# A hybrid DeltaNet and window-attention layer: rounds of an inverse spread over more steps, value copies in two halves, and a lasting slot for wide weights

## The chip, the cores and the metric

One core of one Trainium2 chip runs the whole layer in one launch. The metric is the device time of a run in microseconds (us); the kernel before takes 1549.96 us, the median of 3 runs (1548.43 to 1550.71).

## The reference, cut to what matters

One layer on 1024 latent tokens and 256 context tokens, width 1024, in float32. It projects all tokens once and sends the columns to two groups.

```python
px = modulate(rms_norm(x, norm1_w), sh1, sc1) @ w_in          # latents; pc the same for the context
# group A, gated DeltaNet: short_conv + SiLU on q, k, v; q and k L2-normalised;
#   per head, direction and chunk of 64 tokens a triangular solve, then a scan over chunks
m = where(strict, einsum(kb, k) * decay, 0);  a_mat = I + m
u = triangular_solve(a_mat, v * beta);  w = triangular_solve(a_mat, kb * exp(gam))
# group B, neighbourhood attention on a 16 x 64 grid: q, k RMS-normed per head (weights na_q, na_k);
#   each query sees an 8 x 16 window and all context keys, with a learned 2-D bias
x = x + g1 * (concat(dn_x, na_x) @ w_out)
x = x + g2 * swiglu(modulate(rms_norm(x, norm2_w), sh2, sc2), w_ffn_in, w_ffn_out)
```

## The kernel before, in words

The projection stage, up to about 600 us, is a list of jobs run one behind another. Each job is a group of columns of the input projection, and its matmuls (float32 split in a high and a low part, so three products: hh by whi, hl by whi, hh by wlo) fill TensorE. Then come the scan and the rest of the attention, the output projection and the FFN, which the change does not touch.

There are two kinds of job. A `Block` makes 128 columns over all its tokens: `k`, `q`, `v` of group A, `nk` and `nq` of group B. Its result stands in up to three of four `blk` banks; ScalarE copies it out (`evac`, L438 and L453), VectorE and ScalarE do convolution taps and SiLU (L457 to L468), and `norm` and `finish` do sums over heads and transposes for the next stage. A `Wide` job makes 256 or 272 columns, token tile by token tile: `z1`, `nv0`, `nv1`, and at the end `z0`. Its weights are loaded in two halves through one buffer `wraw`, cast by ScalarE into the tile `zw` (L587).

The jobs in order: k0 to k3, z1, nk0, nk1, nk2, nv0, nk3, q0 to q3, nq0 to nq3, v0, nv1, v1, v2, v3, z0.

Beside the jobs runs a background program (`bg`), which is advanced by one step after each of eight parts of a block's matmuls, and by two or three steps after each tile of a wide job. First it computes the inverses of the triangular 32 x 32 matrices of all chunks (`block_inverses`): thirty rounds on VectorE over a tile `N` (L885 and L887), then transposes of `N` on TensorE (L897), then products that are stored in DRAM as `x_d`. Then come the `preps`, ten of them in eight steps each, which read `x_d` (as `xc`) and the products of keys `kk_d`, and put decay factors (`rg` on GpSimd, L957; `pr` on TensorE, L967) on them. Preps from the third on wait until all q jobs are finished.

The text order is not the engines' order: a scheduler places each engine's instructions by its own rules, so a step that is handed out elsewhere changes what stands in front of what on all five queues. All loads and most stores are issued by SyncE, in the order of its queue.

Three more names. In `norm` of an nk job, a sum over heads (L492) is made in three segments, each followed by Ln on ScalarE (L493); all take a bank of the tag `m`. The normalised nk keys go to DRAM as `nk_d`, the nv values as `nv_d` and from there, copied in window order, as `vw_d` (L1108); v goes to `v_d` (L535). The first attention pair reads `qs`, `kh`, `kl` (L303) and is handed out among the tiles of z0.

Of the kernel before, what the change touches and what calls it, by code (L numbers as in the profile page):

```python
# [20 lines left out]
KT = 8  # L21
# [67 lines left out]
def hybrid(ctx, tc, a, dbg):  # L89
# [45 lines left out]
        dve.memset(bias[:, i:i + 1], v)  # L135
    b_eps, b_naq = bias[:, 0:1], bias[:, 1:2]
    mr = const("mr", [128, 5, 128], F32R)
    mneg = const("mneg", [128, 2, 128], F32R)

    v_d = dram.tile([T, 512], F32, name="v_d", tag="v_d")  # L140
    k_d = dram.tile([T, 512], F32, name="k_d", tag="k_d")
# [233 lines left out]
    with ExitStack() as bs:  # L375
# [32 lines left out]
        class Block:  # L408
# [64 lines left out]
            def norm(self):  # L473

                kind, acc, t0, i = self.kind, self.acc, self.t0, self.i
                if kind == "v":
                    return
                if kind == "k":
                    sp.dma_start(kT_d[:, :, i], acc.rearrange("p (c t) -> p c t", t=128))
                    return  # L480
                r = self.r
                if kind == "q":
                    sp.dma_start(qT_d[:, :, i], acc[:, t0:].rearrange("p (c t) -> p c t", t=128))
                    p = bank()
                    for c in range(8):
                        pe.matmul(p[:, c:c + 1], r[:, t0 + c * 128:t0 + (c + 1) * 128], M[C_ONE][:, 0:1],
                                  start=True, stop=True)
                    dve.tensor_copy(SQ[:, :, i], p[:, 0:8])
                    return
                for s0, n in self.segs:  # L490
                    p = bank()
                    pe.matmul(p[:, :n], M[C_BD2], r[:, s0:s0 + n], start=True, stop=True)  # L492
                    act.activation(r[:, s0:s0 + n], p[:, :n], AF.Ln, bias=b_eps, scale=1.0 / ND)  # L493
                if kind == "nq":
                    act.activation(r[:, t0:], r[:, t0:], AF.Exp, scale=-0.5, bias=b_naq)
                else:
                    act.activation(r[:, t0:], r[:, t0:], AF.Exp, scale=-0.5)
                isk = kind == "nk"
                u = acc
                dve.scalar_tensor_tensor(u[:, t0:], u[:, t0:], qkw[:, isk:isk + 1], r[:, t0:],  # L500
                                         op0=OP.mult, op1=OP.mult)
                hl16 = cp.tile([128, 2, T], F16, name="hl16", tag="kx", bufs=3)
                h16, l16 = hl16[:, 0], hl16[:, 1]
                if isk:
                    act.copy(h16, u)
                    dve.tensor_tensor(l16, u, h16, OP.subtract)
                else:
                    for hf in range(2):
                        s = slice(t0 + hf * 512, t0 + hf * 512 + 512)
                        uv = u[:, s].rearrange("p (r b c) -> p b r c", r=8, b=4)  # L510
                        hv, lv = (x[:, s].rearrange("p (b r c) -> p b r c", b=4, r=8) for x in (h16, l16))
                        act.copy(hv, uv)
                        dve.tensor_tensor(lv, uv, hv, OP.subtract)
                for i, x in enumerate((h16, l16)):
                    for hb in range(2):
                        hd = 2 * self.i + hb
                        dst = nk_d[i, hd] if isk else nq_d[hd, i]
                        sp.dma_start(dst, x[hb * 64:hb * 64 + 64, t0:])

            def finish(self):  # L520
                kind, acc, i = self.kind, self.acc, self.i
                if kind in "kv":
                    vt = cp.tile([128, NCH, 128], F32, name="vt", tag="kx", bufs=3)
                    for g, m in ((0, 4), (4, 4), (8, 2)):
                        p = bank()
                        for c in range(m):
                            pe.transpose(p[:, c * 128:(c + 1) * 128], acc[:, (g + c) * 128:(g + c + 1) * 128], ident)
                        if kind == "k":
                            act.copy(vt[:, g:g + m].rearrange("p c d -> p (c d)"), p[:, :m * 128])
                        else:  # L530
                            dve.tensor_tensor(vt[:, g:g + m], p[:, :m * 128].rearrange("p (c d) -> p c d", d=128),
                                              SV[:, g:g + m, i:i + 1].to_broadcast([128, m, 128]), OP.mult)
                        yield
                    dst = v_d if kind == "v" else k_d
                    sp.dma_start(dst[:, i * 128:(i + 1) * 128].rearrange("(c p) d -> p c d", p=128), vt)  # L535
                if kind == "q":
                    kT = cp.tile([128, T], F32, name="kTh", tag="kx", bufs=3)
                    sp.dma_start(kT.rearrange("p (c t) -> p c t", t=128), kT_d[:, :, i])
# [25 lines left out]
        class Wide:  # L564


            def __init__(self, kind, half, zp):
                self.kind, self.half, self.zp = kind, half, zp
                self.n = 272 if kind == "z" and half else 256
                self.lasting = kind == "z" and not half  # L570

            def room(self):
                w = self.zp().tile([128, 2, KT, 256 if self.lasting else 272], F32R, name="zw", tag="zw")
                self.hi, self.lo = w[:, 0], w[:, 1]

            def prefetch(self):
                h2, n = 2 * self.half, self.n // 2
                src = a["w_nv"] if self.kind == "nv" else a["w_z%d" % self.half]
                if self.kind == "z":
                    h2 = 0  # L580
                if not self.lasting:
                    self.room()
                for i in range(2):
                    raw = wp.tile([128, KT, 136], F32, name="wraw", tag="wraw", bufs=1)
                    r, s = raw[:, :, :n], slice(i * n, i * n + n)
                    sp.dma_start(r, src[h2 + i])
                    act.copy(self.hi[:, :, s], r)  # L587
                    pool.tensor_tensor(self.lo[:, :, s], r, self.hi[:, :, s].bitcast(F32), OP.subtract)
# [55 lines left out]
        with ExitStack() as xs:  # L644
# [65 lines left out]
            with tc.manual_schedule(engines={mybir.EngineType.PE, mybir.EngineType.DVE, mybir.EngineType.Activation}):  # L710
# [30 lines left out]
                for k in range(1, KT):  # L741
# [11 lines left out]
                                ada(q, act.copy)  # L753
                    if k == 5:
                        act.copy(mr[:, 4], ident)
                        for d in range(2):
                            act.mul(mneg[:, d], masks[:, d], -1.0e30)
                        act.copy(mr[:, 0:4], masks)

        cp = pools(bs, "cp", "right")  # L760
        late = ExitStack()
        adp = pools(late, "adp", "left")
        zpool = [pools(late, "zp", "left")]
        first_half = ExitStack()
        cpa = pools(first_half, "cpa", "left")
        WK = cpa.tile([128, 2, NU, 32], F32, name="WK", tag="WK")
        KKc = WK[:, 1]

        def zp():
            return zpool[0]  # L770

        def decay_tables(gp):
            def small(name):
# [51 lines left out]
        def block_inverses():  # L825
            with ExitStack() as gs:
# [55 lines left out]
                for c in range(30, 0, -1):  # L882
# [2 lines left out]
                    dve.tensor_tensor(t, N[:P, :, 0:c, c:c + 1].to_broadcast([P, 4, c, w]),  # L885
                                      N[:P, :, c:c + 1, c + 1:32].to_broadcast([P, 4, c, w]), OP.mult)
                    dve.tensor_tensor(N[:P, :, 0:c, c + 1:32], N[:P, :, 0:c, c + 1:32], t, OP.add)  # L887
                    if c % 2:
                        yield
                flat = N.rearrange("p b r c -> p b (r c)")  # L890
                dve.memset(flat[:P, :, 0:1024:33], 1.0)
                yield
                U = WK.rearrange("p d u i -> p (d u) i")
                for i0 in range(0, 32, 4):
                    p = bank()
# [21 lines left out]
        def preps():  # L917

            first_half.close()
            with ExitStack() as gs:  # L920
# [28 lines left out]
                def prep(i, got):  # L949
# [9 lines left out]
                    for d, c, kk, xc, at in got:  # L959
                        for q in q32:  # L960
                            act.copy(fxs[d][q, :, q], xc[q, 1])
                    yield 1
                    es = []
                    for d, c, kk, xc, at in got:
                        p = bank("pr")
# [61 lines left out]
                        yield  # L1027
                flush(tick[0] + 2)

        jobs = first + [Block("k", 2), Block("k", 3), Wide("z", 1, zp)]  # L1030
        inv = len(jobs)
        jobs += [Block("nk", i) for i in range(3)] + [Wide("nv", 0, zp), Block("nk", 3)]
        turn = len(jobs)
        jobs += [Block("q", i) for i in range(4)]
        later = len(jobs)
        queries = range(turn, later)
        jobs += [Block("nq", i) for i in range(4)] + [Block("v", 0), Wide("nv", 1, zp)]
        values = len(jobs) - 1
        jobs += [Block("v", i) for i in (1, 2, 3)] + [Wide("z", 0, zp)]

        def blk(n):
            return jobs[n] if 0 <= n < len(jobs) and isinstance(jobs[n], Block) else None
# [9 lines left out]
        for n in range(2, len(jobs) + 2):  # L1052
# [7 lines left out]
            if n == len(jobs) - 2:  # L1060
                bg.drain()
                bg2.drain()
                late.close()
                sp1 = pools(middle, "sp1", "left")
                zpool[0] = sp1
                jobs[n + 1].room()
                fill = attention(pools(attn, "nw", "left", 2))
                next(fill)
            if final:
# [21 lines left out]
            elif j:  # L1091
                for k in range(KT):
                    j.mm([k])
                    if k >= 3:
                        next(fin, 0)
                    bg.step(1)
                    if n > inv + 4:
                        bg2.step(1)
# [1 line left out]
            for _ in fin:  # L1100
                pass
            done.add(n - 2)
            if isinstance(j, Wide) and n == values:
                vlat = nv_d[CT:].rearrange("(r c) d -> r c d", c=64)
                for cb in range(4):
                    for ch in range(4):
                        for r in range(4):
                            sp.dma_start(vw_d[r * 32:r * 32 + 32, :, cb, ch],  # L1108
                                         vlat[4 * ch + r, BLKS[cb]:BLKS[cb] + 32].rearrange("c (h d) -> c h d", d=128))
            if nrm:  # L1110
                nrm.norm()
            if isinstance(j, Block):
# [665 lines left out]
```

## Time and profile before

| | |
|---|---|
| median of 3 runs | 1549.96 us |
| profiled execution | 1549.54 us |
| its span | 1547.5 us |
| TensorE busy | 1479.8 us (96%) |
| VectorE, ScalarE, GpSimd busy | 994.3, 727.7, 233.6 us |
| inverse's rounds on VectorE | to 258.5 us |
| q0 to q3 | 249.6 to 342.8 us |
| nv1 | 437.7 to 494.6 us |
| v1, v2, v3 | 496.6 to 548.5 us |

The time of a run is that of the span and 2.0 us around it. In the rows of the profile a row begins with the line of the kernel and the engine, `out<-in` are the names of the tiles, and the arrow in brackets names what ended the idle time in front of an instruction.

### The profile page before, as it was taken

The page shows a single profiled execution, that of the slowest core. Times are in us where ns is not written, and L with a number is a line of the kernel's source. Part 1 is how long each engine was busy: PE and PEld are TensorE (multiplying, and loading weights), DVE is VectorE, ACT ScalarE, POOL GpSimd, SP SyncE. Part 2 cuts the span into 40 slices and gives each one's busy share as a digit, 9 for nine tenths or more (in the row PEclk, how much of TensorE's full clock was granted, in tenths as well). Part 3 has the DMA queues.
Part 4 walks back from the last instruction along what each step waited for, and adds up shares of the span by engine and source line. Part 5 has one row for each costly group of instructions (what it writes and reads, how often), then busy time and mean ns, then how long its engine had stood idle before and what let it go on. Part 6 is the DMA issues. An engine that isn't in the chain of part 4 may idle for free. (4 is left out here: it accounts for less than half of the span.)

```text
span 1547.5 us, 23963 instructions
## 1 busy us (share of the span) xinstructions
PE 1479.8 (96%) x8702; PEld 1235.2 (80%) x8702; DVE 994.3 (64%) x1712; ACT 727.7 (47%) x1404; POOL 233.6 (15%) x286
## 2 busy tenths in 40 slices
PE   6999999899989978999999999999999999999998
PEld 3788787678778867888887878888888888888887
DVE  5774497675554543777986469866665556599652
ACT  5442552635764235666773166333333334354440
POOL 1154500733554010111210000000000000000000
PEclk9999999999999979999999999999999999999999
DMA  9274221577556467899637502632323324698742
GB/s 389 64 217 133 67 72 63 163 212 241 182 169 212 130 174 237 283 288 261 220 102 255 208 34 82 211 102 103 103 102 103 109 100 159 231 381 279 244 144 82
DMA packets 204118, 267.35 MB, mean 173 GB/s; under 512 B 16736, under 2 KB 114528, under 8 KB 202976
## 3 DMA queue, kind: packets, MB, share of 16 engines
q1 hardware_dynamic: 198480, 261.07, 51.7%
q10 hardware_dynamic: 5520, 4.76, 0.9%
q8 instruction: 68, 1.11, 0.3%
q14 instruction: 50, 0.41, 0.1%
HBM read 201.02 MB, written 68.94 MB: 174 GB/s over the span
## 5 line engine op out<-in xcount | busy, mean ns | idle before, releaser
L405 PE MATMUL blk<-hh,whi 128*128 128x512 f32 (+1 forms) x410 | 123.4, 395 | 2.3 <-ACT kk L550 1.4
L1415 ACT CAST uhi<-wq 128x512 fp32r<-128x512 f32 x101 | 61.0, 622 | 133.5 <-issue 84.6
L1415 ACT CAST uhi<-ws 128x512 fp32r<-128x512 f32 x91 | 53.9, 621 | 147.3 <-PE ps L1354 92.9
L405 PE MATMUL blk<-hl,whi 128*128 128x512 f32 (+1 forms) x410 | 116.8, 377 | 0.3 <-DVE hl L707 0.3
L595 PE MATMUL blk<-zw,hh 128*128 128x256 f32 (+1 forms) x576 | 115.0, 293 | 1.3 <-ACT kk L550 1.1
L405 PE MATMUL blk<-hh,wlo 128*128 128x512 f32 (+1 forms) x410 | 114.7, 377 | 0.6 <-POOL wlo L200 0.6
L1416 DVE TENSOR_TENSOR ulo<-wq,uhi 128x512 fp32r<-128x512 f32 x101 | 67.4, 687 | 59.1 <-ACT uhi L1415 34.0
L1354 PE MATMUL ps<-hT,uhi 128*128 128x512 f32 x336 | 103.7, 390 | 0.0
L1354 PE MATMUL ps<-hT,ulo 128*128 128x512 f32 x336 | 103.5, 389 | 0.0
L1354 PE MATMUL ps<-lT,uhi 128*128 128x512 f32 x336 | 103.4, 389 | 0.0
L595 PEld LDWEIGHTS blk<-zw,hh 128*128 128x128 f32 x576 | 92.8, 192 | 5.2 <-ACT kk L550 1.4
L1354 PE MATMUL ps<-hB,uhi 128*128 128x512 f32 x288 | 89.2, 391 | 0.6 <-ACT hB L1529 0.6
L1354 PE MATMUL ps<-lB,uhi 128*128 128x512 f32 x288 | 88.7, 389 | 0.4 <-DVE lB L1530 0.4
L1354 PE MATMUL ps<-hB,ulo 128*128 128x512 f32 x288 | 88.7, 389 | 0.0
L405 PEld LDWEIGHTS blk<-hh,wlo 128*128 128x128 f32 x410 | 72.6, 192 | 15.3 <-POOL wlo L200 0.9
L405 PEld LDWEIGHTS blk<-hl,whi 128*128 128x128 f32 x410 | 72.4, 191 | 14.5 <-DVE hl L707 0.8
L405 PEld LDWEIGHTS blk<-hh,whi 128*128 128x128 f32 x410 | 69.4, 194 | 18.2 <-issue 4.5
L595 PE MATMUL blk<-zw,hl 128*128 128x256 f32 (+1 forms) x288 | 83.2, 289 | 0.0
L1354 PEld LDWEIGHTS ps<-lT,uhi 128*128 128x128 f32 x336 | 63.1, 188 | 13.1
L1354 PEld LDWEIGHTS ps<-hT,ulo 128*128 128x128 f32 x336 | 63.1, 188 | 13.1
L1354 PEld LDWEIGHTS ps<-hT,uhi 128*128 128x128 f32 x336 | 62.9, 188 | 13.0
L200 POOL TENSOR_TENSOR wlo<-wraw,whi 128x1024 fp32r<-128x1024 f32 x18 | 44.7, 2485 | 179.2 <-ACT whi L199 160.7
(359 smaller groups left out, 3540.5 us busy)
## 6 DMA issues: line engine op xcount, KB each, us to landing
wq<-w_fo SPq DMA_DIRECT2D x99, 256.0 KB, 4.2
wq<-w_gu SPq DMA_DIRECT2D x88, 256.0 KB, 2.9
wad<-wa SPq DMA_DIRECT2D x64, 256.0 KB, 4.4
bt<-rpb SPq DMA_DIRECT2D x64, 192.0 KB, 3.8
t_d<-g SPq DMA_DIRECT2D x22, 512.0 KB, 3.6
fr<-t_d SPq DMA_DIRECT2D x44, 256.0 KB, 5.0
f_d<-g SPq DMA_DIRECT2D x33, 256.0 KB, 2.1
fr<-f_d SPq DMA_DIRECT2D x33, 256.0 KB, 3.8
```

Of the source, the lines that this page charges most:

```text
L200: lo_engine.tensor_tensor(o, r, h.bitcast(F32), OP.subtract)
L405: pe.matmul(o, ww[:, k], xx[k][:, s], start=k == 0 and j == 0, stop=k == KT - 1 and j == 2)
L595: pe.matmul(p[:, :c1 - c0], x[k][:, s], ww[:, k, c0:c1], start=k == 0 and j == 0, stop=k == KT - 1 and j == 2)
L1354: pe.matmul(o, w[wi][:, k], x[xi][:, k], start=first and k == 0 and j == 0, stop=k == n - 1 and j == 2, skip_group_check=True)
L1415: act.copy(hi, self.raw[key])
L1416: dve.tensor_tensor(lo, self.raw[key], hi.bitcast(F32), OP.subtract)
```

## The change

Eight edits. (1) The rounds of the inverse are handed out one a step, not two. (2) Four empty steps, in place of one, stand before the transposes of `N`, and the first prep gets one empty step before its first sums. (3) In `norm`, the third segment's sum takes a bank of the tag `pr`. (4) The copies to `vw_d` are made in two halves, one of two heads behind nv0 and one behind nv1, each of 64 copies. (5) The store of `v_d` is issued by ScalarE. (6) The tile `zw` is taken from a pool that lasts, opened early, always at its full width. (7) The product `mneg` is made later, in another pool. (8) The last `finish` of the q jobs marks its job done as soon as its steps are through.

```diff
                 for j, (s0, n) in enumerate(self.segs):
-                    p = bank()
+                    p = bank("pr" if j == 2 else "m")
...
-                    sp.dma_start(dst[:, i * 128:(i + 1) * 128].rearrange("(c p) d -> p c d", p=128), vt)
+                    (act if kind == "v" else sp).dma_start(dst[:, i * 128:(i + 1) * 128].rearrange("(c p) d -> p c d", p=128), vt)
...
             def room(self):
-                w = self.zp().tile([128, 2, KT, 256 if self.lasting else 272], F32R, name="zw", tag="zw")
+                w = sp1.tile([128, 2, KT, 272], F32R, name="zw", tag="zw")
...
-                if not self.lasting:
-                    self.room()
+                self.room()
...
+        sp1 = pools(middle, "sp1", "left")
         adp = pools(late, "adp", "left")
-        zpool = [pools(late, "zp", "left")]
+        mneg = adp.tile([128, 2, 128], F32R, name="mneg", tag="mneg")
+        for d in range(2):
+            act.mul(mneg[:, d], mr[:, d].bitcast(F32), -1.0e30)
...
-                    if c % 2:
-                        yield
+                    yield
                 flat = N.rearrange("p b r c -> p b (r c)")
                 dve.memset(flat[:P, :, 0:1024:33], 1.0)
-                yield
+                for _ in range(4):
+                    yield
...
                     yield 1
+                    if i == 0:
+                        yield 1
...
-                    if k >= 3:
-                        next(fin, 0)
+                    if k >= 3 and next(fin, 0) == 0:
+                        done.add(n - 2)
...
-            if isinstance(j, Wide) and n == values:
+            if isinstance(j, Wide) and j.kind == "nv":
+                hv = slice(2 * j.half, 2 * j.half + 2)
...
-                            sp.dma_start(vw_d[r * 32:r * 32 + 32, :, cb, ch],
-                                         vlat[4 * ch + r, BLKS[cb]:BLKS[cb] + 32].rearrange("c (h d) -> c h d", d=128))
+                            rows = vlat[4 * ch + r, BLKS[cb]:BLKS[cb] + 32].rearrange("c (h d) -> c h d", d=128)
+                            sp.dma_start(vw_d[r * 32:r * 32 + 32, hv, cb, ch], rows[:, hv])
```

What moves, first on SyncE's queue around nv0. Before, with the load of q2's weights (`wraw<-w_conv`) in the fifth row:

```order
L518 DMA nk_d<-hl_1621 64x1280 x4
L195 DMA wraw<-w_conv 128x8x128
L518 DMA nk_d<-hl_1794 64x1280 x4
L518 DMA nk_d<-hl_1992 64x1280 x4
L195 DMA wraw<-w_conv 128x8x128
L907 DMA x_d<-WK 128x1280
L910 DMA x_d<-ut 128x1280
```

And now the same place, from q1's weights on:

```order
L194 DMA wraw<-w_conv 128x8x128
L517 DMA nk_d<-hl_1788 64x1280 x4
L1104 DMA vw_d<-nv_d 32x2x128 x22
L517 DMA nk_d<-hl_1970 64x1280 x2
L1104 DMA vw_d<-nv_d 32x2x128
L517 DMA nk_d<-hl_1970 64x1280 x2
L1104 DMA vw_d<-nv_d 32x2x128 x41
L194 DMA wraw<-w_conv 128x8x128
L902 DMA x_d<-WK 128x1280
L194 DMA wraw<-w_conv 128x8x128
L905 DMA x_d<-ut 128x1280
```

All 64 copies of the first half stand in front of q2's weights and of the first `x_d` store, and q3's weights between the two `x_d` stores.

Then ScalarE's queue from v1's evacuation (`cr<-blk`) on. Before:

```order
L453 COPY cr<-blk 128x512 x2
L1001 COPY y_2232<-pr 32x4x96
L468 ACT_TABLE_LOAD
L468 ACTIVATE cacc<-cacc 128x1280
L453 COPY cr<-blk 128x256
L453 COPY cr<-blk 128x512 x2
L468 ACTIVATE cacc<-cacc 128x1280
L453 COPY cr<-blk 128x256
L453 COPY cr<-blk 128x512 x2
L587 CAST zw<-wraw 128x8x128
```

Now:

```order
L452 COPY cr<-blk 128x512 x2
L584 CAST zw<-wraw 128x8x128
L467 ACT_TABLE_LOAD
L467 ACTIVATE cacc<-cacc 128x1280
L452 COPY cr<-blk 128x256
L452 COPY cr<-blk 128x512 x2
L467 ACTIVATE cacc<-cacc 128x1280
L584 CAST zw<-wraw 128x8x128
L534 DMA v_d<-vt 128x10x128
L452 COPY cr<-blk 128x256
L452 COPY cr<-blk 128x512 x2
```

The first cast of z0's weights stood behind v3's evacuation; it stands now between v1's and v2's, and the store of `v_d` has come to this queue.

Last, TensorE at the end of v3 (the last `blk<-` of L405 before, L404 now). Before:

```order
L405 MATMUL blk<-hh_458,wlo 128x256
L405 MATMUL blk<-hh_458,wlo 128x512 x2
L303 LDWEIGHTS qs
L303 MATMUL sc<-kh,qs 128x256
L303 LDWEIGHTS qs
L303 MATMUL sc<-kh,qs 128x256
```

Now:

```order
L404 MATMUL blk<-hh_457,wlo 128x256
L404 MATMUL blk<-hh_457,wlo 128x512 x2
L592 MATMUL blk<-zw,hh_128 128x256
L592 MATMUL blk<-zw,hl_129 128x256
L592 MATMUL blk<-zw,hh_128 128x256
L592 MATMUL blk<-zw,hh_130 128x256
```

The first scores of the attention (`sc`) came right behind v3; now 96 matmuls of z0, four token tiles, stand between.

More of the change, by code (lines that the diff above doesn't have):

```diff
@@ L137, in hybrid @@
     mr = const("mr", [128, 5, 128], F32R)
-    mneg = const("mneg", [128, 2, 128], F32R)
     v_d = dram.tile([T, 512], F32, name="v_d", tag="v_d")
@@ L489, in norm @@
                     return
-                for s0, n in self.segs:
-                    p = bank()
+                for j, (s0, n) in enumerate(self.segs):
+                    p = bank("pr" if j == 2 else "m")
                     pe.matmul(p[:, :n], M[C_BD2], r[:, s0:s0 + n], start=True, stop=True)
@@ L564, in hybrid, with __init__ @@
         class Wide:
-            def __init__(self, kind, half, zp):
-                self.kind, self.half, self.zp = kind, half, zp
+            def __init__(self, kind, half):
+                self.kind, self.half = kind, half
                 self.n = 272 if kind == "z" and half else 256
-                self.lasting = kind == "z" and not half
             def room(self):
-                w = self.zp().tile([128, 2, KT, 256 if self.lasting else 272], F32R, name="zw", tag="zw")
+                w = sp1.tile([128, 2, KT, 272], F32R, name="zw", tag="zw")
                 self.hi, self.lo = w[:, 0], w[:, 1]
@@ L755, in hybrid @@
                         act.copy(mr[:, 4], ident)
-                        for d in range(2):
-                            act.mul(mneg[:, d], masks[:, d], -1.0e30)
                         act.copy(mr[:, 0:4], masks)
@@ L767, in hybrid @@
         KKc = WK[:, 1]
-        def zp():
-            return zpool[0]
         def decay_tables(gp):
@@ L1028, in preps @@
                 flush(tick[0] + 2)
-        jobs = first + [Block("k", 2), Block("k", 3), Wide("z", 1, zp)]
+        jobs = first + [Block("k", 2), Block("k", 3), Wide("z", 1)]
         inv = len(jobs)
-        jobs += [Block("nk", i) for i in range(3)] + [Wide("nv", 0, zp), Block("nk", 3)]
+        jobs += [Block("nk", i) for i in range(3)] + [Wide("nv", 0), Block("nk", 3)]
         turn = len(jobs)
@@ L1036, in hybrid @@
         queries = range(turn, later)
-        jobs += [Block("nq", i) for i in range(4)] + [Block("v", 0), Wide("nv", 1, zp)]
+        jobs += [Block("nq", i) for i in range(4)] + [Block("v", 0), Wide("nv", 1)]
         values = len(jobs) - 1
-        jobs += [Block("v", i) for i in (1, 2, 3)] + [Wide("z", 0, zp)]
+        jobs += [Block("v", i) for i in (1, 2, 3)] + [Wide("z", 0)]
         def blk(n):
@@ L1063, in hybrid @@
                 late.close()
-                sp1 = pools(middle, "sp1", "left")
-                zpool[0] = sp1
-                jobs[n + 1].room()
                 fill = attention(pools(attn, "nw", "left", 2))
```

## The prediction

> **What bounds the kernel now.** The page comes first: TensorE is busy for nearly the whole span.
>
> ```profile
> span 1547.5 us, 23963 instructions
> PE 1479.8 (96%) x8702; PEld 1235.2 (80%) x8702; DVE 994.3 (64%) x1712; ACT 727.7 (47%) x1404; POOL 233.6 (15%) x286
> ```
>
> So time is won or lost only as TensorE idle time (67.7 us in all) or as a lower granted clock. Busy time by stretches says where (start:end, length, PE busy, then the other engines, PEclk, DMA share, GB/s):
>
> ```profile
> 140.00:260.00 120.00, 109.54 (x638) 92.93 (x637) 91.29 (x112) 49.64 (x79) 35.29 (x27) 0.98 0.21 60
> 260.00:345.00 85.00, 77.42 (x437) 61.93 (x436) 53.91 (x51) 42.71 (x73) 39.12 (x42) 0.89 0.56 176
> 345.00:497.00 152.00, 143.28 (x1045) 119.31 (x1044) 84.49 (x106) 90.24 (x169) 72.69 (x88) 1.00 0.66 205
> 497.00:612.00 115.00, 98.71 (x679) 83.47 (x678) 52.35 (x83) 44.83 (x79) 12.27 (x21) 0.90 0.58 171
> ```
>
> The change moves nothing outside 140 to 612 us that TensorE waits for. Idle in the four stretches: 10.5, 7.6, 8.7 and 16.3 us. The clock takes (1 - 0.89) x 85 = 9.4 us in 260:345 and 0.10 x 115 = 11.5 us in 497:612. What TensorE waits for, in windows 140:300, 300:500 and 500:612 (total us, times, longest):
>
> ```profile
> PE m L492 <- ACT cr L493: 5.3, 4, 1.4
> PE pr L967 <- POOL rg L957: 2.9, 3, 1.2
> PE m L897 <- DVE N L891: 2.9, 1, 2.9
> ...
> PE pr L998 <- DVE y L1000: 1.9, 1, 1.9
> PE m L219 <- DVE acc L234: 1.5, 1, 1.5
> ...
> PE sc L303 <- DVE mx L305: 5.1, 2, 4.1
> PE sc L303 <- DMA kh<-nk_d: 4.5, 1, 4.5
> ...
> ```
>
> The short waits cost more than their length, since half clock follows some of them. The first of these stretches begins right behind the wait of 1.5 us (L219), the second in the wait for kh; the clock is the third number from the end:
>
> ```profile
> 330.50:333.80 3.30, 3.30 (x9) 2.62 (x10) 3.14 (x5) 0.00 (x0) 0.00 (x0) 0.50 0.81 242
> 552.40:569.30 16.90, 9.71 (x43) 7.54 (x44) 11.95 (x18) 6.74 (x10) 3.06 (x3) 0.50 0.87 246
> ```
>
> I price such a stretch at 1.7 us (half of some 3.3), or at 3.4 where the wait is long enough for two of them. The Trainium skill (TensorE: Matmul & The Clock Gate, HAM oscillation) says that it takes an idle gap of over some 3.4 us to lose the clock. The rows disagree: 1.5 us was enough once. By that rule the query stretch would lose no clock, before or after, except behind the one wait of 5 us below, and the sum would be about 1.7 us worse than mine.
>
> **Part 1, nk sums and the inverse (140 to 260 us).** The third of three sums (L492) gets a bank of its own and no longer waits for the Ln of the first: 5.3 us in four places, three of them before 235 us (4.0 us), one at 273. But behind them stands L897, which waits for VectorE, and VectorE has no room:
>
> ```profile
> 196.00:258.00 62.00, 56.48 (x368) 49.75 (x366) 59.38 (x63) 23.93 (x34) 5.46 (x2) 1.00 0.21 60
> ```
>
> Its 59.4 busy us of 62 are the rounds of the inverse, instruction after instruction, and their order is unchanged. Only the first of the four waits lies before the rounds begin, so the rounds end at most 1.3 us earlier; I take 1.2. The transposes also come three 512-column matmuls later in TensorE's row, 0.7 us of work that now covers part of their wait. **Gain 1.9 us**, not 4.0; the wait at L897 itself grows.
>
> **Part 2, queries (260 to 345 us).** Splitting the values puts 64 more copies vw_d<-nv_d behind nv0. There are still 64 of them behind nv1, each half as large: 128 copies in place of 64. SyncE's price for issuing one (ns min/median/max):
>
> ```profile
> L1108 SPq DMA_DIRECT2D vw_d<-nv_d x64: 469/596/1811, 461.0 to 531.4; - x64
> L940 SPq DMA_DIRECT2D kk<-kk_d x20: 320/462/1326, 285.1 to 482.0; - x20
> L195 SPq DMA_DIRECT2D wraw<-w_conv x10: 540/593/658, 32.8 to 442.0; - x10
> 525.61 6.36 SPq L1108 DMA_DIRECT2D vw_d<-nv_d  x10
> ```
>
> In a row they come every 0.64 us (ten in 6.36). What half a copy costs no row shows. The bounds are 0.47 (its own minimum; kk's median is 0.46) and 0.64. Issue time does not follow size: 512 KB of wraw take 593 ns, 64 KB of vw_d 596, 256 KB of kk 462. So I take **0.64, the price of a whole one**; the lower end is a rival. In the new order q2's weights wait for all 64:
>
> ```profile
> nv_d<-zt ACTq DMA_DIRECT2D x20, 128.0 KB, 2.3
> wraw<-w_conv SPq DMA_DIRECT2D x10, 512.0 KB, 3.8
> ...
> 236.12 0.33 ACTq L606 DMA_DIRECT2D nv_d<-zt  x1
> ...
> 253.36 0.59 SPq L195 DMA_DIRECT2D wraw<-w_conv  x1
> 269.49 1.04 ACT L199 CAST whi<-wraw 128x1024 fp32r<-128x1024 f32 x1 [4.61 <-PE blk L405]
> 270.44 1.07 ACT L453 COPY cr<-blk 128x512 f32<-128x512 f32 x2
> 270.61 2.37 POOL L200 TENSOR_TENSOR wlo<-wraw,whi 128x1024 fp32r<-128x1024 f32 x1 [17.27 <-ACT whi L199]
> 271.54 4.77 DVE L457 TENSOR_SCALAR cacc<-cr,cw 128x1024 f32<-128x1024 f32 x1 [3.59 <-ACT cr L453]
> 284.99 2.05 DVE L461 SCALAR_TENSOR_TENSOR cacc<-cr,cw,cacc 128x1022 f32<-128x1022 f32 x1
> ...
> 273.84 1.92 POOL L931 MEMSET y<- 128x512 f32 x4
> ...
> 269.02 0.39 PE L405 MATMUL blk<-hl,whi 128*128 128x512 f32 x1
> 269.24 0.62 PE L405 MATMUL blk<-hh,wlo 128*128 128x512 f32 x2
> ...
> 275.22 1.28 ACT L497 ACT_TABLE_LOAD   x1
> ```
>
> The last store of nv0 is issued at 236.1, about 3.0 earlier with part 1 (4.0 of waits gone, 1.0 given back to an earlier transpose that waits for VectorE), and lands 2.3 later: 235.4. The first block of sixteen copies waits for that one; 49 copies remain, 49 x 0.64 = 31.4, and four nk_d stores stand among them, 2.4 at the same price. The load goes out at 269.2 instead of 253.4 and lands at 273.0. ScalarE's cast of it stood at 269.5, or 267.6 with part 1: **5.4 us late**, and everything queued behind it on ScalarE with it: the evacuation cr<-blk of q0, the Ln of the sums, then on VectorE the taps, on GpSimd wlo and rg. The three places where TensorE meets this chain, in its new order:
> - L219, 30 matmuls into q1. Matmuls of 512 columns start every 0.23 us (two of 0.39 in 0.62), so 7 us after q1's start at some 268.6 (270.6 less 1.9): 275.6. It needs a bank that the Ln frees: cast at 273.0 (1.0), two copies (1.1), table load (1.3), two Ln (1.1): 277.5, or 1 us more with the third: **2 to 4 us late**, 3 taken.
> - L486 (q0's squares) has moved to 8 matmuls into q2. Before, the taps ran from 271.5 to 287.0, 15.5 us, 3 of them for two other steps of the inverse that now come later. So 12.5 from 275.5, then table load, silu and square (1.3 + 1.1 + 1.1): 291.5 at most, and 288.5 if wlo disturbs the first tap less than before. TensorE is there at 278.6 + 4.2 (the rest of q1) + 1.9 = 284.7: 4 to 6.5 us; 5 taken.
> - L967 (first preps) has moved from the end of q1 to 22 matmuls into q2, but GpSimd now makes q3's wlo (2.4) and six memsets (2.9) before rg's four pieces. 2 to 5 us; 3 taken, in place of the 2.9.
>
> New waits 11; old ones that go 1.3 + 2.9 + 1.5 and, taken half, 1.9: 6.6. One half-clock stretch more: 1.7. **Loss 6.1 us** (3 to 9). The mask product computed earlier (mneg) and the four empty steps cost nothing: GpSimd, ScalarE and the steps' owners have slack there, and the work is the same.
>
> **Part 3, 345 to 497 us.** Preps 2 to 9 start later and end three steps earlier. The same instructions meet 8.7 us of idle; **0, at most 3 either way**.
>
> **Part 4, values to the first attention pair (497 to 612 us).**
>
> ```profile
> 495.00 0.33 ACTq L606 DMA_DIRECT2D nv_d<-zt  x1
> ...
> 535.68 0.61 SPq L586 DMA_DIRECT2D wraw<-w_z  x1
> 545.47 0.37 SPq L535 DMA_DIRECT2D v_d<-vt  x1
> ...
> 532.78 1.35 ACT L453 COPY cr<-blk 128x256 f32<-128x256 f32 x3 [3.34 <-PE blk L405]
> ...
> 541.09 1.27 ACT L468 ACTIVATE cacc<-cacc 128x1280 f32<-128x1280 f32 x1 [6.96 <-DVE cacc L461]
> ...
> 549.35 1.07 ACT L587 CAST zw<-wraw 128x1024 fp32r<-128x1024 f32 x1
> ...
> wraw<-w_z SPq DMA_DIRECT2D x1, 512.0 KB, 4.7
> ```
>
> Before, SyncE sat from 536.3 to 545.5 waiting to store v_d, and kh came late behind it: the 4.5 us. Now that store is ScalarE's, and z0's first half stands ahead of the first pair in TensorE's row, so the 4.5 goes, and of the waits for mx behind it I keep 2.0. The new wait: ScalarE's first zw cast has moved ahead of the evacuation of v2, and it needs w_z. That load stands behind 48 copies that need the last nv_d: 495.0 + 2.3 + 48 x 0.64 + 1 (two stores among them) + 3.7 (the six stores from 532.0 to 535.7) = 532.7, landed at 537.4. Cast 1.1, table load 1.3, silu 1.3, first copy 0.4: 541.5. TensorE is done with v2 as its evacuation starts, at 533, and v3 needs v2's banks: **8.5 us of stall**, and 3.4 for the clock behind it. Clock in the pair 1.7 (8.5 before). The pair's idle time is 16.9 - 9.7 = 7.2 in the row of half clock above and 3.9 of the 4.5 that lie before it; the rest of the stage, 5.2 idle and 3.0 clock, stays. Sum 8.5 + 3.4 + 2.0 + 1.7 + 8.2 = 23.8 against 16.3 + 11.5 = 27.8: **gain 4.0 us** (0 to 8). The moved store of v_d stands on ScalarE ahead of v3's evacuation; what it stores is v1's, finished while v3 runs, so it holds nothing up (at worst 1 to 2 us, since two of v3's three banks are read behind it).
>
> **Sum** against the profiled execution, 1549.54 us (span 1547.5 and 2.0 around it; the median is 0.4 more): -1.9 + 6.1 + 0 - 4.0 = +0.2. Forecast **1550 us**, no change, by two large terms that cancel; its own range is 1543 to 1557.
>
> **The rivals.**
> - *The half copies issue at 0.48.* For: kk's and vw_d's own shortest. Against: the median, and that wraw, eight times the size, costs the same. Then q2's load goes out 49 x 0.16 = 7.8 earlier, in time for the cast, and the three new waits fall to what stood there before (part 2: 0). w_z lands 7.7 earlier, the stall falls to 0.8 without its clock, and part 4 gains 4.0 + 7.7 + 3.4 = 15.1. With part 1, 17 less; I take 15 to 16, **1534 us**. It decides from about 0.55 downward.
> - *SyncE's queue is slower than the steady pace, and each wait behind it draws half clock.* For: the 64 copies hold outliers up to 1.8 us, 1.2 over the median. Against: the median is at the steady pace. Two such outliers in each run of 48 put 2.4 on q2's load and 2.4 on w_z, and two more half-clock stretches cost 3.4: 8.2 more, **1558 us**. It decides from a mean of 0.69 upward, seen as waits at L486 and at v3's first matmul of over 7 and 10 us.
> - *The change does nothing that TensorE sees* (banks and queues give way elsewhere): within 3 us of before, part of the forecast.
>
> **How the numbers follow.** Forecast 0.50, fast copies 0.22, slow queue 0.28. The range reaches to both rivals, 1536 to 1560. A measurement of this kernel tells 0.2%, 3.1 us, from no change. Of the forecast's 0.50 I put 0.14 under 1546.9, 0.21 within and 0.15 over. Faster 0.36, same 0.21, slower 0.43.
>
> **What would show it.** Right: L492 gone from the waits; L897's wait over 3.5 us; vw_d's median issue near 600 ns with 128 of them; new waits at L486 and L219 (their lines shifted by a few) of 3 to 6 us; a stall of 8 to 9 us between v2 and v3 released by ScalarE's evacuation; no wait for kh. Wrong: a vw_d median under 530 ns, or no stall at v3, makes it 10 to 15 us faster; a wait at the second w_z half, or preps that end later than nv1, makes it slower than all of this.

## The result, and the profile after

The changed kernel takes 1541.36 us, the median of 20 runs, against 1549.66 us: 0.9952 of before, 95% interval 0.9941 to 0.9963. It is 8 us faster where no change was forecast. In the profiled execution, 1541.49 us, the page begins:

```profile
span 1539.4 us, 24029 instructions
PE 1474.1 (96%) x8702; PEld 1231.0 (80%) x8702; DVE 993.6 (65%) x1712; ACT 728.2 (47%) x1405; POOL 234.8 (15%) x286
```

The stretches of before, in the same columns (length, PE busy, the other engines, then PEclk, DMA share, GB/s), and one more:

```profile
140.00:260.00 120.00, 109.50 (x642) 92.93 (x641) 92.12 (x115) 49.59 (x78) 35.36 (x27) 0.97 0.26 73
260.00:345.00 85.00, 80.58 (x467) 64.25 (x466) 64.93 (x57) 44.90 (x76) 41.69 (x42) 0.94 0.66 203
345.00:497.00 152.00, 143.80 (x1062) 119.91 (x1062) 75.17 (x102) 95.43 (x180) 74.41 (x95) 0.98 0.64 196
497.00:612.00 115.00, 101.37 (x741) 87.42 (x740) 52.73 (x95) 45.76 (x91) 12.00 (x16) 0.97 0.59 172
612.00:915.00 303.00, 293.91 (x2249) 251.14 (x2248) 212.11 (x565) 177.97 (x443) 32.64 (x65) 1.00 0.67 209
```

The queries lose 4.4 us to waits (7.6 before) and 0.06 x 85 = 5.1 to the clock (9.4 before). From v1 to the first attention pairs it is 13.6 (16.3) and 3.5 (11.5); some of that moved on, since 612:915 holds 9.1 us of idle time where before held 5.1. Counted between the same matmuls instead: from nk0's first to v2's last 387.0 us (391.6), from there to the scan's first product with `vk` (L1229, L1234 before) 74.7 (78.3). So 4.6 us came from the part up to v2's last matmul and 3.6 from the part behind it.

What TensorE waits for in 140:260, 260:345 and 500:612:

```profile
PE m L892 <- DVE N L885: 5.7, 1, 5.7
...
PE pr L964 <- POOL rg L952: 2.7, 4, 0.9
PE pr L984 <- DVE kk L971: 1.1, 1, 1.1
PE m L485 <- ACT cr L470: 0.2, 1, 0.2
...
PE blk L404 <- ACT cr L452: 5.3, 1, 5.3
PE sc L313 <- DVE bt L308: 2.6, 2, 1.8
```

The sums are gone and the wait for the rounds has grown to 5.7. The waits of 3 and 5 us forecast among the queries are not there (0.2 at L485). The new stall at v3 is there, 5.3 us and not 8.5. SyncE's and ScalarE's timelines around nv0 and q2's weights, and SyncE's price of a copy (ns min/median/max), say why:

```profile
215.42 14.71 SPq L1104 DMA_DIRECT2D vw_d<-nv_d  x22
...
231.46 0.64 SPq L1104 DMA_DIRECT2D vw_d<-nv_d  x1
...
233.42 27.31 SPq L1104 DMA_DIRECT2D vw_d<-nv_d  x41
260.83 0.59 SPq L194 DMA_DIRECT2D wraw<-w_conv  x1
...
234.83 0.37 ACT L602 COPY zt<-blk 128x256 f32<-128x256 f32 x1 [3.48 <-DMA vw_d<-nv_d]
238.06 0.34 ACTq L603 DMA_DIRECT2D nv_d<-zt  x1
...
269.17 1.05 ACT L198 CAST whi<-wraw 128x1024 fp32r<-128x1024 f32 x1 [0.58 <-PE blk L404]
...
L1104 SPq DMA_DIRECT2D vw_d<-nv_d x128: 529/595/1690, 215.4 to 521.3; - x128
```

A half copy costs what a whole one did (595 and 596 ns), as forecast. But 23 of the 64 go out while nv0 still runs, and the others do not wait for the last store at 238.06. The load goes out at 260.8, and ScalarE's cast of it waits for TensorE, not for the load. The last store itself did not come 3.0 us earlier, as forecast, but 1.9 later than before (236.12): the profile has ScalarE wait 3.48 us, in front of the copy that feeds it, for the landing of copies to `vw_d`. No wait of TensorE in 140:260 is put down to that. The end of nv1 and v3, on both queues:

```profile
490.92 30.98 SPq L1104 DMA_DIRECT2D vw_d<-nv_d  x46
...
525.45 0.61 SPq L583 DMA_DIRECT2D wraw<-w_z  x1
...
530.57 1.05 ACT L584 CAST zw<-wraw 128x1024 fp32r<-128x1024 f32 x1 [13.89 <-DMA wraw<-w_z]
531.64 1.28 ACT L467 ACT_TABLE_LOAD   x1
532.93 1.27 ACT L467 ACTIVATE cacc<-cacc 128x1280 f32<-128x1280 f32 x1
534.11 1.33 ACT L452 COPY cr<-blk 128x256 f32<-128x256 f32 x3
```

The chain is the forecast one (46 copies, load, cast, table, silu, first copy of v2's banks), only it begins at 490.9 and not behind the last nv_d store, forecast to land at 497.3. The 46 copies take 0.67 us each, under the 0.69 from which the rival of the slow queue decides.

### The profile page after: what moved, and what is told of

Read it like the earlier page. It is cut to its first block, busy times and chain, and to the rows that moved or that the text cites. A ratio compares the mean times of both kernels' runs of the same rounds, so it can differ in the third digit from the quotient of the medians.

```text
span 1539.4 us, 24029 instructions
## 1 busy us (share of the span) xinstructions
PE 1474.1 (96%) x8702; PEld 1231.0 (80%) x8702; DVE 993.6 (65%) x1712; ACT 728.2 (47%) x1405; POOL 234.8 (15%) x286
## 5 line engine op out<-in xcount | busy, mean ns | idle before, releaser
L404 PE MATMUL blk<-hh,whi 128*128 128x512 f32 (+1 forms) x410 | 123.0, 394 | 6.8 <-ACT cr L452 5.3
L404 PE MATMUL blk<-hl,whi 128*128 128x512 f32 (+1 forms) x410 | 115.4, 375 | 0.3 <-DVE hl L704 0.3
L404 PE MATMUL blk<-hh,wlo 128*128 128x512 f32 (+1 forms) x410 | 114.6, 375 | 0.6 <-POOL wlo L199 0.6
L404 PEld LDWEIGHTS blk<-hh,whi 128*128 128x128 f32 x410 | 69.0, 194 | 21.9 <-ACT cr L452 6.1
L404 PEld LDWEIGHTS blk<-hl,whi 128*128 128x128 f32 x410 | 72.5, 192 | 14.9 <-DVE hl L704 0.8
L404 PEld LDWEIGHTS blk<-hh,wlo 128*128 128x128 f32 x410 | 72.5, 192 | 14.9 <-POOL wlo L199 0.9
```

The source lines that it names most:

```text
L404: pe.matmul(o, ww[:, k], xx[k][:, s], start=k == 0 and j == 0, stop=k == KT - 1 and j == 2)
```

## The experiments

All are timed against before; the changed kernel stands at 0.9952. The first four undo one edit each.

**The bank of the third sum** (`x_pr`): `bank("pr" if j == 2 else "m")` becomes `bank()`.

> The changed kernel with one edit undone: the third sum of norm takes a bank of the tag m again. Theory A (the gain in front of v2's end, 4.6 us, comes mostly from the background steps being handed out later; three of the four waits at the sums are swallowed by the wait for the inverse's rounds): the four waits of 1.2 to 1.4 us come back, the wait for the rounds shrinks by as much, 1 to 2 us slower than the changed kernel, ratio to before 0.996. Rival B (the bank is the gain there): 4 to 5 us slower, ratio 0.998.

1541.91 us, 0.9953 (0.9935 to 0.9972). Theory A, since B's 0.998 lies outside. Its waits in 140:300:

```profile
PE m L491 <- ACT cr L492: 5.2, 4, 1.4
...
PE m L892 <- DVE N L885: 2.2, 1, 2.2
```

The 5.2 us of sums come back, and the wait for VectorE's rounds falls from 5.7 to 2.2. The bank is worth nothing that these runs can tell.

**The steps** (`x_yield`):

```diff
-                    yield
+                    if c % 2:
+                        yield
...
-                for _ in range(4):
-                    yield
+                yield
...
-                    if i == 0:
-                        yield 1
```

> The changed kernel with the steps undone: two rounds of the inverse a step, one empty step in front of its transposes, none in front of the first sums. Theory A: the transposes stand earlier in TensorE's row and wait longer, the first preps fall into the q jobs with waits at rg and y and a half-clock stretch more, 3 to 5 us slower than the changed kernel, ratio 0.998. Rival B (the bank): 0 to 1 us slower, ratio 0.9955.

1547.99 us, 0.9993 (0.9975 to 1.0012): 6.6 us slower than the changed kernel, more than theory A's 3 to 5. Its stretches:

```profile
140.00:260.00 120.00, 107.77 (x635) 91.90 (x635) 92.02 (x114) 48.77 (x76) 35.18 (x27) 0.97 0.26 73
260.00:345.00 85.00, 79.78 (x442) 63.55 (x441) 50.43 (x46) 45.89 (x79) 49.43 (x58) 0.90 0.63 195
345.00:497.00 152.00, 142.52 (x1060) 119.13 (x1060) 82.63 (x109) 93.44 (x174) 65.21 (x77) 0.99 0.64 198
```

1.7, 0.8 and 1.3 us more idle, and the clock among the queries at 0.90 instead of 0.94, 3.4 us. So the steps do it and not the bank; but the waits that theory A names hardly differ (at the transposes 6.5 us and 5.7 in the changed kernel, at `rg` 2.9 and 2.7), and which wait makes the loss is not shown.

**The split** (`x_nosplit`):

```diff
-            if isinstance(j, Wide) and j.kind == "nv":
-                hv = slice(2 * j.half, 2 * j.half + 2)
+            if isinstance(j, Wide) and n == values:
+                hv = slice(0, 4)
```

> The changed kernel with the value copies in one go behind nv1 again, 64 whole ones; its order puts the first attention pair ahead of z0 as before and the first zw cast behind v2's evacuation. Theory A (the split acts by the order that the scheduler makes of it, not by what SyncE does with it): the 5.3 us stall at v3 goes, and waits and half clock at the first attention pair come back, 3 to 5 us slower than the changed kernel, ratio 0.998. Rival C (the split only adds 64 issues): the stall goes and nothing comes back, 4 to 6 us faster than the changed kernel, ratio 0.992.

1548.09 us, 1.0001 (0.9984 to 1.0019). Theory A, rather stronger than expected: 6.7 us slower than the changed kernel. The stall at v3 is gone; in 500:612 stands instead

```profile
PE sc L302 <- DVE mx L304: 8.1, 2, 7.1
PE sc L313 <- DVE bt L308: 4.1, 3, 2.5
...
545.34 5.90 DVE L460 SCALAR_TENSOR_TENSOR cacc<-cr,cw,cacc 128x255 f32<-128x255 f32 x6
551.16 0.82 DVE L304 CUSTOM_DVE_ANT_0 bt<-sc,bt 128x640 f32<-128x640 f32 x1
```

The last two rows, of VectorE's timeline, say what the pair waits for: its first softmax step (L304) stands behind v3's taps (L460), and TensorE has no z0 in hand meanwhile.

**The store of v_d** (`x_vd`): `(act if kind == "v" else sp)` becomes `sp`.

> The changed kernel with v_d stored by SyncE again; in its order v1's store stands behind twelve loads of the first attention pairs. Theory A: nothing of the first pair waits for it, within 2 us of the changed kernel, ratio 0.995. Rival D (moving that store is what freed kh): a wait for kh or a late second half of w_z, 4 us or more slower, ratio 0.998.

1535.92 us, 0.9917 (0.9892 to 0.9942). Both were wrong: it is 5.4 us *faster* than the changed kernel. ScalarE's timeline:

```profile
515.49 1.28 ACT L467 ACT_TABLE_LOAD   x1
524.33 1.27 ACT L467 ACTIVATE cacc<-cacc 128x1280 f32<-128x1280 f32 x1 [7.56 <-DVE cacc L460]
530.01 1.05 ACT L584 CAST zw<-wraw 128x1024 fp32r<-128x1024 f32 x1 [4.40 <-DMA wraw<-w_z]
530.96 1.34 ACT L452 COPY cr<-blk 128x256 f32<-128x256 f32 x3
```

Without the stores on its queue the scheduler puts the cast behind v1's table load and silu, which no longer stand between the load and v2's copies: a stall of 3.4 us at v3, not 5.3. The other part lies behind v3, where the waits in 500:640 add up to 6.7 us instead of 10.9 without that stall. The order of ScalarE's queue differs there too: in the changed kernel the pair's third softmax step (`bt`, 573.93) stands behind a copy that waits 3.06 us for TensorE, in `x_vd` (567.71) ahead of it.

**One edit alone, on the kernel before** (`b_split`, `b_yield`, `b_vd`, the same lines the other way round).

> The kernel before with the value copies in two halves, nothing else. Its order puts 104 rows of z0 ahead of the first attention pair, as in the changed kernel, and v_d stays on SyncE. Theory A (the split acts by that order): the waits and the half clock at the first pair go, a stall of some 3 us at v3 comes; 5 to 8 us faster than before, ratio 0.996. Rival C (the split needs the lasting slot, or is paid back at q2's weights): within 2 us of before, ratio 1.000.

1543.01 us, 0.9948 (0.9931 to 0.9965). Theory A: **the split alone gives as much as the whole change**, but not in the same places (table below). In 260:345 and 497:612 it shows

```profile
260.00:345.00 85.00, 77.90 (x437) 62.09 (x437) 55.75 (x52) 42.26 (x71) 40.35 (x42) 0.90 0.61 189
497.00:612.00 115.00, 101.66 (x740) 87.28 (x738) 52.34 (x88) 45.91 (x91) 12.71 (x22) 0.96 0.58 172
```

The queries are as before (77.4 busy, 0.89); the 64 copies ahead of them show no cost there. Behind v1 there are 3.0 us less idle and 0.06 x 115 = 6.9 us less lost to the clock.

> The kernel before with the steps alone: one round of the inverse a step, four empty steps, one empty step in front of the first sums. Theory A (the steps act by themselves): 5 to 6 us faster than before, all of it between 260 and 530 us, ratio 0.9965. Rival E (they gain only because the split's copies delay the first preps' loads): within 2 us of before, ratio 1.000.

1547.75 us, 0.9982 (0.9965 to 1.0000). Between the two: 2.4 us by the medians, 0 to 5.4 by the interval.

> The kernel before with the store of v_d issued by ScalarE, nothing else. The prediction's step: SyncE no longer waits for that store, kh comes 9 us earlier, the wait of 4.5 us for it goes: 3 to 5 us faster than before, ratio 0.997. Rival D (the store costs on ScalarE what x_vd showed, 5 us): slower by 2 us and more, ratio 1.002.

1551.54 us, 1.0014 (0.9999 to 1.0029). The prediction's step is wrong: its 3 to 5 us lie outside the interval (rival D's 2 us and more is not settled). The wait for kh goes, but another takes its place. Waits of SyncE in 530:565 and of TensorE in 500:612, then VectorE's timeline:

```profile
SPq L262 <- DMA v_d<-vt: 8.1, 1, 8.1
...
PE sc L303 <- DMA bt<-rpb: 7.1, 1, 7.1
...
549.97 5.89 DVE L461 SCALAR_TENSOR_TENSOR cacc<-cr,cw,cacc 128x255 f32<-128x255 f32 x6
555.78 0.82 DVE L305 CUSTOM_DVE_ANT_0 bt<-sc,bt 128x640 f32<-128x640 f32 x1
```

SyncE is not free: its fourth load of kh now waits 8.1 us for that store to land. And the scores, which begin earlier (548.3, before 553.0), meet VectorE in v3's taps. The wait of 7.1, before a matmul at 556.66, is put down to loads of `bt`, but the two for this pair had landed by 553.5; what ends just before it, at 556.6, is the first softmax step, behind those taps. Before, the waits were 4.5 for kh and then 4.1 for this step.

The three alone multiply to 0.9948 x 0.9982 x 1.0014 = 0.9944, beside 0.9952 for all of them. On that count nothing that these runs can tell is left for the lasting slot, `mneg` and the earlier mark, which no run undoes. Where each edit acts shows when the profiled executions, one of each kernel, are counted between the same matmuls (us):

| kernel | nk0's first to v2's last | from there to the first `vk` |
|---|---|---|
| before | 391.6 | 78.3 |
| `b_yield` | 385.1 | 77.2 |
| `b_split` | 393.4 | 71.8 |
| `b_vd` | 390.4 | 81.9 |
| changed | 387.0 | 74.7 |
| `x_yield` | 391.7 | 75.7 |
| `x_nosplit` | 386.1 | 81.9 |
| `x_vd` | 386.8 | 68.4 |

The steps act in front of v2's end (4.7 to 6.5 us less). The split acts behind it (6.5 to 7.2 less), and so does the store of v_d (3.6 to 6.3 more).

**Half of the steps** (`x_rounds`: the empty steps undone, the rounds one a step kept).

> The changed kernel with the rounds one a step, but one empty step in front of the transposes and none in front of the first sums. Theory A: the fifteen further steps carry the gain, the four empty ones little, within 2 us of the changed kernel, ratio 0.996. Rival F (the empty steps keep the transposes from TensorE while VectorE is late): the wait at the transposes grows by 2 us and more, ratio 0.998.

1545.31 us, 0.9973 (0.9955 to 0.9991). Between the changed kernel and `x_yield`. Neither fits: it is 4.0 us slower than the changed kernel, not within 2, and the wait at the transposes is 6.4 us, 0.7 longer and not 2. The time does not say how much each kind of step carries.

**Toward a faster kernel.** `x_vdmerge` has v_d on SyncE and four copies made one:

```diff
                     for ch in range(4):
-                        for r in range(4):
-                            rows = vlat[4 * ch + r, BLKS[cb]:BLKS[cb] + 32].rearrange("c (h d) -> c h d", d=128)
-                            sp.dma_start(vw_d[r * 32:r * 32 + 32, hv, cb, ch], rows[:, hv])
+                        for h in (2 * j.half, 2 * j.half + 1):
+                            rows = vlat[4 * ch:4 * ch + 4, BLKS[cb]:BLKS[cb] + 32, h * 128:h * 128 + 128]
+                            sp.dma_start(vw_d[:, h, cb, ch].rearrange("(r c) d -> c r d", c=32),
+                                         rows.rearrange("r c d -> c r d"))
```

> The changed kernel with v_d stored by SyncE and the value copies merged four and four in one head each, 32 behind each nv job in place of 64 (same bytes, 64 KB each). Theory A (a copy costs SyncE some 0.6 us whatever its size): w_z is loaded 7 us earlier, the stall of 3.4 us at v3 and its half clock go, 4 to 6 us faster than with v_d alone moved back, ratio 0.988. Rival G (issue follows size): 1.2 us a copy and no gain, ratio 0.9917.

1529.68 us, 0.9865 (0.9843 to 0.9886). Theory A. A copy of twice the size costs the same, w_z goes out some 10 us earlier than in the changed kernel, counted from nk0, and the stall is 0.4 us (tile, SyncE's timeline, waits):

```profile
L1104 SPq DMA_DIRECT2D vw_d<-nv_d x64: 528/599/1405, 213.8 to 499.3; - x64
...
512.69 0.61 SPq L583 DMA_DIRECT2D wraw<-w_z  x1
...
PE blk L404 <- ACT cr L452: 0.4, 1, 0.4
```

`x_best_yield` undoes the steps in it.

> The kernel with merged copies and v_d on SyncE (x_vdmerge), with the steps undone as in x_yield: two rounds a step, one empty step, none in front of the first sums. Theory A (the steps gain wherever the split stands): 5 to 7 us slower than x_vdmerge, ratio 0.9905. Rival H (the 6.6 us of x_yield were the lot of its half-clock stretches; alone the steps gain 2 to 3): ratio 0.9885.

1539.31 us, 0.9932 (0.9918 to 0.9945): 9.6 us slower than `x_vdmerge`, above theory A's 5 to 7. Rival H falls: its 0.9885 lies outside the interval.

`x_best_e8` has `range(8)` in place of `range(4)` empty steps.

> x_vdmerge with eight empty steps in front of the transposes of the inverse instead of four, 24 matmuls of q0 and q1 more ahead of them. Theory A (TensorE waits there for VectorE's rounds, 4.8 us and half clock behind, with other work at hand): the wait goes, the preps still end in front of v2, 4 to 8 us faster than x_vdmerge, ratio 0.983. Rival I (the first preps come later by as much and wait for xc and rg instead): within 2 us of x_vdmerge, ratio 0.9865.

**1525.99 us, 0.9844 (0.9825 to 0.9863)**: the fastest, 24 us under before. The waits in 140:345, first of `x_vdmerge`, then of this kernel:

```profile
PE m L892 <- DVE N L885: 4.8, 1, 4.8
```

```profile
PE m L892 <- ACT WK L894: 0.8, 1, 0.8
PE m L892 <- ACT cr L492: 0.5, 1, 0.5
```

TensorE has matmuls of q0 to do until the rounds are through. Theory A by sign and by the wait; the two intervals overlap, so the gain over `x_vdmerge`, 3.7 by the medians, is not settled closely. Its profiled execution is a fast one, 5.4 us under the median.

## Why the prediction was wrong

*The sum* forecast a loss of 4.2 us up to v2's end (parts 1 to 3) and a gain of 4.0 behind it; the runs showed a gain of 4.6 and one of 3.6. So the sign was lost in the first of these.

*Part 1* held in mechanism: the sums' 5.3 us are mostly swallowed by the wait for the rounds (`x_pr`), and that wait came out over 3.5 us. Its gain of 1.9 is not told from nothing: `x_pr` is 0.6 us slower.

*Part 2* failed, and with it the sign. The step is "The first block of sixteen copies waits for that one; 49 copies remain". I put the whole queue behind nv0's last store, while the scheduler puts the copies whose rows are ready in front: 23 were out by 232 us. The load was forecast for 269.2 and went at 260.8; the 5.4 us of lateness, and the waits of 3 (L219) and 5 us (L486) that hung on it, did not come; the one at `rg` came, 2.7 for 3 taken, but it had been 2.9 before. `b_split`, which has all 64 copies there, shows the queries as they were before, so no loss of 6.1 is seen. The order that I had quoted showed these copies split 22, 1 and 41 around the nk_d stores. It could have told me.

The same part said that the four empty steps "cost nothing" and looked for no gain in the steps. By the medians they gave 2.4 us alone, 6.6 in the changed kernel and 9.6 beside merged copies. Up to v2's end they take off 6.5, 4.7 and 6.0 us (390.7 to 384.7 in the last), though the execution of `b_yield` is 8.6 under its median. So where they act is shown, in less idle time and less half clock; that they are worth more beside the split is not, nor which wait they shorten.

*Part 4* was right in mechanism: z0 ahead of the first pair takes away its waits and half clock, and a stall at v3 takes their place. The term that was mis-sized is that stall, 5.3 and not 8.5, from the same wrong start of the queue. The store of v_d was the second error: "it holds nothing up" looked only at v1's store between two casts. In the changed kernel it costs 5.4 us, as far as the rows tell by the order that comes of it on ScalarE; and moved alone it does not win the 4.5 us of kh, since VectorE's taps are the next thing to wait for. That part 4 still came out at 3.6 for 4.0 is luck: a stall 3.2 too long stood against a store priced at nothing.

The prices of single instructions were right, the copy's above all (595 ns), which rules out the rival of fast copies: the kernel became faster, but not by that. What was wrong is where things stand and when they may start.

## What to carry to other kernels

With a list scheduler, an edit acts by the order that comes of it as much as by its own cost: the split bought no time on SyncE, and its gain shows where z0's matmuls came ahead of the first attention pair. (No run moves z0 alone: without the split the store of v_d also stood ahead of loads of that pair on SyncE, or held them up.) When a batch of copies is put behind a producer, ask for each copy what it reads before costing the queue from the last store. A store moved to another queue still has to land for whoever waits for it, and a wait taken away may only show the next one. Where an engine must wait anyway, handing it other work in front (the steps) was worth more here than taking away waits ahead of it (the bank).

## What the runs showed of the hardware

SyncE takes 0.6 us to issue one of these copies whether it moves 32 KB (595 ns), 64 KB of one row of tokens and four heads (596) or 64 KB of four rows and one head (599). For these copies the count matters, not the bytes.

Waits under 3.4 us cost clock again. In the changed kernel the waits in 345:500 are at most 2.1 us, and yet the clock is 0.60 soon behind one of them (waits, TensorE's timeline, and a stretch):

```profile
PE pr L995 <- ACT kk L987: 7.3, 6, 2.1
...
397.24 0.25 PE L995 MATMUL pr<-y,kk 128*32 128x32 f32 x2 [2.01 <-ACT kk L987]
...
398.50:402.00 3.50, 3.50 (x11) 2.74 (x10) 1.29 (x2) 3.38 (x9) 0.00 (x0) 0.60 0.32 72
```

The Trainium skill (TensorE: Matmul & The Clock Gate, HAM oscillation) puts the limit at gaps of over some 3.4 us; this case's rows do not bear that out.

Runs of one kernel also spread more than most edits here are worth, and the granted clock goes with them, roughly: 29 runs of before lie between 1539.1 us at a mean clock of 0.993 and 1554.4 at 0.984. One profile is one draw from that: the one of `b_yield` took 1539.2 us (median 1547.8), that of `x_rounds` 1549.5 (median 1545.3), so these two profiles alone would rank the kernels the wrong way round.
